# Keeping the two short row blocks of a softmax in the score bank

## The chip, the cores and the metric

The kernel runs on one core of a Trainium2 chip. Five engines work side by side, each through its own instruction queue: TensorE (PE, matrix products and transposes), VectorE (DVE), ScalarE (ACT), GpSimd (POOL) and SyncE (SP, which here issues nearly all transfers from memory). Matrix products land in eight accumulator banks, each 128 partitions by 512 float32 columns; everything else lies in SBUF, the on-chip memory. DVE and ACT can read and write both; POOL touches SBUF alone in this kernel.

The metric is the device time of one execution in microseconds (us). An execution can also be profiled: the profiler then gives the start and the duration of every instruction, and what released each wait.

## The reference

The model is a two-layer decoder trunk on one sequence of 512 tokens, width 1024, with 16 heads of 64 columns. Each layer is an attention block, an output projection with a normalisation, and a gated feed-forward block. The first layer uses a stick-breaking attention, the second a "forgetting" attention, a causal softmax with a learned decay:

```
for blk in range(s_len // Q_BLOCK):           # blocks of 128 queries
    z = einsum('bhqd,bhkd->bhqk', qb, kb) * scale
    decay = cum[:, :, q0:k_end, None] - cum[:, :, None, :k_end]
    logits = where(s_idx <= t_idx, z + decay, -inf)
    p = softmax(logits, axis=-1)
    outs.append(einsum('bhqk,bhkd->bhqd', p, vb))
```

Block `blk` sees 128, 256, 384 or 512 keys, because the attention is causal. The results must agree with float32 arithmetic; the kernel therefore splits operands of its products into a high and a low part, and a projection multiplies three times.

## The kernel before

The attention of a layer is one loop over 17 steps, `attention`. Step h computes scores and probabilities of head h and, at the same time, transposes the probabilities of head h - 1 and multiplies them with its values. Within a step the four query blocks go from the longest row (512 columns) to the shortest (128). Between these pieces PE gets other work in fixed portions, the "filler": the projections of the next heads' queries, keys and values (tiles `pqk` and `pv`), and in the last four steps the first part of the output projection (tile `po`, lines 266 to 268), whose sums stay in banks until the attention is over: two banks for each of the first two row blocks, and two more for the third.

The order of PE and of SP is the order of the program text, written by hand. The order on ACT, DVE and POOL is worked out by a planner when the program is built, from its own estimates of durations. On the chip each engine runs its list strictly in order, and an instruction that waits holds up everything behind it on its engine.

All eight banks come from one ring (tile tag `bank`). A bank is given out again when the last instruction that reads its content is done. SBUF tiles of 512 columns come from a pool of 44 slots (`slot`).

The parts that matter here:

- `scores` (line 388) fills a bank `ps` with the scores of one row block, two products.
- `fox` (lines 403 to 413) makes probabilities of it. DVE adds the decay `cum`, finds the extreme value of each row (`mx`) and writes the sum to an SBUF slot `fx` (line 407). ACT takes the exponential in place in `fx` and sums each row (line 410, the sum is read out by a second small instruction). DVE takes the reciprocal (line 411) and scales `fx` in place (line 412).
- `transposed` (line 422) turns the four blocks by PE into banks `pa`; ACT writes the rounded high part `ah`, DVE the remainder `al` (lines 192 and 193).
- `weighted` (lines 437 and 438) multiplies `ah` and `al` with the values into a bank `po`. ACT and DVE fold its halves together (lines 442 and 443).
- `queries` (lines 359 and 361) and `keys` (lines 377 to 380) prepare the next pair of heads on ACT, DVE and POOL; POOL also makes the low parts of the weights (`wl`, `sl`, line 193) and masks the decay (`cum`, line 502).
- `stick` is the first layer's counterpart of `fox`. There, too, the rows of up to `MULN` = 256 columns stay in their bank (`om = slot("om", F32) if n > MULN else ps`), and DVE's last product on line 400 reads the bank; for the longer rows POOL makes that product, from SBUF.

Of the kernel before, what the change touches and what calls it, by code (L numbers as in the profile page):

```python
# [8 lines left out]
F32 = mybir.dt.float32  # L9
F32R = mybir.dt.float32r  # L10
BF16 = mybir.dt.bfloat16
AF = mybir.ActivationFunctionType
ALU = mybir.AluOpType
AX = mybir.AxisListType

P = 128
# [12 lines left out]
MULN = 256  # L29
# [8 lines left out]
def trunk(ctx, tc, x, c, w_mod, b_mod, g_mix_pre, g_mix_post, w_qkv, w_o, w_fg, b_fg,  # L38
          g_ffn_pre, g_ffn_post, w_gate, w_up, w_conv, b_conv, w_down, out):
    nc = tc.nc  # L40
# [6 lines left out]
    def nm(s):  # L47
        serial[0] += 1
        return f"{s}_{serial[0]}"
# [4 lines left out]
    def slot(s, dt=F32R):  # L54
        return sb.tile([P, 512], dt, tag="slot", name=nm(s), bufs=NS)
# [7 lines left out]
    def tiny(s, n=1):  # L63
        return sb.tile([P, n], F32, tag=f"tiny{n}", name=nm(s), bufs=24)
# [336 lines left out]
        return bt  # L401

    def fox(ps, qb, cum):
        n = (qb + 1) * P
        t = slot("fx", F32)
        m, s, r = tiny("mx"), tiny("sm"), tiny("rc")
        nc.vector.tensor_tensor_reduce(
            t[:, :n].rearrange("p (b k) -> p b k", k=P), ps[:, :n].rearrange("p (b k) -> p b k", k=P), cum(qb),
            1.0, BIG, op0=ALU.add, op1=ALU.min, accum_out=m)
        nc.scalar.activation(t[:, :n], t[:, :n], AF.Exp, scale=-1.0, bias=m, accum_out=s)  # L410
        nc.vector.reciprocal(r, s)
        nc.vector.tensor_scalar(t[:, :n], t[:, :n], r, None, op0=ALU.mult)
        return t

    def transposed(probs):
# [111 lines left out]
    def attention(l, qk, vt, ot, filler, units, bg):  # L527
# [4 lines left out]
        for h in range(NH + 1):  # L532
# [17 lines left out]
            for qb in range(NT - 1, -1, -1):  # L550
                if h < NH:
                    ps, n = scores(l, hd, qb, qk[p, 0], qk[p, 1])
                    probs[qb] = stick(ps, n) if l % 2 == 0 else fox(ps, qb, cums[h])
                    fill()
                if turned:
                    at = next(turned)
                    fill()
# [207 lines left out]
    for l in range(DEPTH):  # L765
        bg = Background([(l, GT_A), (l, SC_F), (l, SH_F)] if l == 0 else [])
        scale = -0.125 if l % 2 else 0.125
# [174 lines left out]
```

## Time and profile before

| quantity | value |
|---|---|
| median of 3 runs | 1309.29 us (1306.78 to 1309.57) |
| the profiled execution's own time | 1307.82 us |
| its span, first to last instruction | 1306.0 us |
| busy share of the span: PE, DVE, ACT, POOL | 96%, 63%, 47%, 21% |
| the second layer's softmax, first to last reduction (line 407) | 711.8 to 899.9 us |

The span is what the profile divides into engines and lines; the 1.8 us that the profiled execution's time has beyond it are its start and end. The profiled execution is 1.5 us below the median of the runs.

In the listings below a row of the timeline gives start, duration, engine, line, operation, the tile written and the tiles read, the shape, and in square brackets the idle time of that engine before it and who ended it. PE's products overlap: a row of 0.39 us is followed by the next start after some 0.23 us.

### The profile page before, as it was taken

To read this page: it belongs to the slowest core of one execution; us is meant where nothing else is said; L and a number is where in the kernel's file an instruction comes from. 1 tells how busy PE (TensorE), PEld (TensorE's weight loads), DVE (VectorE), ACT (ScalarE), POOL (GpSimd) and SP (SyncE) were. 2 spreads that over 40 slices of the span, in tenths; PEclk is the share of its full clock that TensorE was granted. 3 is DMA by queue.
4 is the path that set the end of the run, shared out by engine and by line. 5 is a ranking of instruction groups with operands and counts; after the bars stand their busy time and mean duration, and the time that the engine had idled before them with its cause. 6 is when DMAs were issued, how large, how long until landed. Compare 5 with 4: busy or idle time off the path is not lost.

```text
span 1306.0 us, 17087 instructions
## 1 busy us (share of the span) xinstructions
PE 1249.1 (96%) x6244; PEld 1050.2 (80%) x6244; DVE 818.9 (63%) x1447; ACT 620.0 (47%) x1182; POOL 277.2 (21%) x302
## 2 busy tenths in 40 slices
PE   5898988999999999999999899999999999999997
PEld 3676867789888888888887788887898888888886
DVE  7778888856878887422264776886775444443233
ACT  5576665757433333311365565566753333332121
POOL 3665444530000000000114554443100000000000
PEclk8999989999999999999999999999999999999999
DMA  8662534231577776333503423232263333333331
GB/s 265 208 193 82 168 107 133 94 108 43 189 242 242 246 229 202 97 97 97 164 1 115 130 91 120 81 129 81 66 210 113 97 97 98 97 97 97 97 97 65
DMA packets 174856, 169.19 MB, mean 130 GB/s; under 512 B 6936, under 2 KB 151728, under 8 KB 174772
## 3 DMA queue, kind: packets, MB, share of 16 engines
q1 hardware_dynamic: 174596, 168.04, 41.1%
q8 instruction: 49, 0.80, 0.3%
q14 instruction: 35, 0.29, 0.1%
q10 hardware_dynamic: 176, 0.07, 0.0%
HBM read 165.92 MB, written 2.16 MB: 129 GB/s over the span
## 4 chain that ended last, share of the span: by engine, by line
PE 72%; DVE 14%; ACT 5%; DMA 4%; issue 3%; POOL 1%; SPq 0%; DVEq 0%; POOLq 0%; ACTq 0%
PE pgu L267 11%; PE pgu L268 11%; PE pgu L266 11%; PE pd L268 6%; PE pd L267 6%; PE pd L266 6%; PE pqk L266 2%; DVE acc L143 2%; PE pqk L267 2%; PE pqk L268 2%; PE po L266 2%; PE po L268 2%; PE po L267 2%; PE ps L388 2%; DMA wm<-in_w_mod_dram 2%
## 5 line engine op out<-in xcount | busy, mean ns | idle before, releaser
L192 ACT CAST wh<-wf 128x1024 fp32r<-128x1024 f32 (+2 forms) x178 | 185.3, 1041 | 319.7 <-PE pgu L267 144.0
L193 DVE TENSOR_TENSOR wl<-wf,wh 128x1024 fp32r<-128x1024 f32 x122 | 149.3, 1224 | 217.9 <-ACT wh L192 215.7
L267 PE MATMUL pgu<-htl,wh 128*128 128x512 f32 (+1 forms) x736 | 276.4, 375 | 0.1
L266 PE MATMUL pgu<-hth,wh 128*128 128x512 f32 (+1 forms) x736 | 276.4, 375 | 0.0
L268 PE MATMUL pgu<-hth,wl 128*128 128x512 f32 (+1 forms) x736 | 276.2, 375 | 0.0
L193 POOL TENSOR_TENSOR wl<-wf,wh 128x1024 fp32r<-128x1024 f32 (+3 forms) x56 | 132.5, 2370 | 131.6 <-ACT wh L192 126.4
L267 PEld LDWEIGHTS pgu<-htl,wh 128*128 128x128 f32 x736 | 138.5, 188 | 25.6 <-DVE htl L328 0.5
L268 PEld LDWEIGHTS pgu<-hth,wl 128*128 128x128 f32 x736 | 138.5, 188 | 25.1
L266 PEld LDWEIGHTS pgu<-hth,wh 128*128 128x128 f32 x736 | 138.5, 188 | 24.9
L279 POOL TENSOR_TENSOR r<-v,mhalf 128x1 f32<-128x1 f32 x32 | 17.9, 558 | 447.3 <-DVE v L275 447.3
L266 PE MATMUL pd<-wh,yh 128*128 128x512 f32 x288 | 112.0, 389 | 0.0
L267 PE MATMUL pd<-wl,yh 128*128 128x512 f32 x288 | 112.0, 389 | 0.0
L268 PE MATMUL pd<-wh,yl 128*128 128x512 f32 x288 | 112.0, 389 | 0.0
L143 DVE SCALAR_TENSOR_TENSOR acc<-wm,csil,acc 128x1024 f32<-128x1024 f32 x74 | 99.4, 1344 | 17.1 <-DMA wm<-in_w_mod_dram 16.8
L266 PE MATMUL pqk<-hth,wh 128*128 128x512 f32 (+1 forms) x240 | 101.5, 423 | 0.1
L268 PE MATMUL pqk<-hth,wl 128*128 128x512 f32 (+1 forms) x240 | 94.5, 394 | 0.3 <-POOL wl L193 0.3
L267 PE MATMUL pqk<-htl,wh 128*128 128x512 f32 (+1 forms) x240 | 94.1, 392 | 0.0
L854 ACT ACTIVATE cv<-cv 128x512 f32<-128x512 f32 x44 | 27.8, 632 | 102.7 <-DVE cv L853 98.2
L266 PE MATMUL pv<-wh,hth 128*128 128x256 f32 (+1 forms) x224 | 70.7, 316 | 1.2 <-ACT wh L192 0.8
L267 PE MATMUL pv<-wl,hth 128*128 128x256 f32 (+1 forms) x224 | 67.7, 302 | 1.2 <-POOL wl L193 1.2
L268 PE MATMUL pv<-wh,htl 128*128 128x256 f32 (+1 forms) x224 | 67.9, 303 | 0.0
L266 PEld LDWEIGHTS pd<-wh,yh 128*128 128x128 f32 x288 | 54.1, 188 | 11.3
(194 smaller groups left out, 2459.6 us busy)
## 6 DMA issues: line engine op xcount, KB each, us to landing
wm<-in_w_mod_dram SPq DMA_DIRECT2D x80, 512.0 KB, 4.8
wf<-in_w_ffn_gate_dram SPq DMA_DIRECT2D x44, 512.0 KB, 4.2
wf<-in_w_ffn_up_dram SPq DMA_DIRECT2D x44, 512.0 KB, 3.7
wf<-in_w_ffn_down_dram SPq DMA_DIRECT2D x44, 512.0 KB, 3.5
wf<-in_w_qkv_dram SPq DMA_DIRECT2D x41, 512.0 KB, 3.8
wm<-in_w_mod_dram SPq DMA_DIRECT2D x32, 256.0 KB, 4.3
wf<-in_w_o_dram SPq DMA_DIRECT2D x16, 512.0 KB, 3.8
cum<-cumd SPq DMA_DIRECT2D x16, 512.0 KB, 4.3
```

Of the source, the lines that this page charges most:

```text
L143: nc.vector.scalar_tensor_tensor(acc, w, csil[:, d : d + 1], acc, op0=ALU.mult, op1=ALU.add)
L192: nc.scalar.copy(hi, src)
L193: (engine or nc.vector).tensor_tensor(lo, src, hi.bitcast(F32), op=ALU.subtract)
L266: nc.tensor.matmul(ps, ah, bh, start=first, stop=False)
L267: nc.tensor.matmul(ps, ah, bl, start=False, stop=False)
L268: nc.tensor.matmul(ps, al, bh, start=False, stop=last)
L279: nc.gpsimd.tensor_tensor(r, v, mhalf, op=ALU.pow)
L388: nc.tensor.matmul(ps[:, :n], q[hd][:, qs], k[hd][i][:, :n], start=i == 0, stop=i == 1)
L854: nc.scalar.activation(a, a, AF.Silu)
```

## The change

`fox` gets a second name, `e`, for the place where the sum and the exponential are written. For rows of 512 and 384 columns it is the SBUF slot as before; for rows of 256 and 128 columns it is the score bank itself. DVE's reduction then writes its sum back to the bank it read, ACT's exponential runs in place in the bank, and DVE's scaling reads the bank and writes the SBUF slot.

```diff
     def fox(ps, qb, cum):
+
         n = (qb + 1) * P
-        t = slot("fx", F32)
+        t = slot("fx", F32)[:, :n]
+        e = t if n > MULN else ps[:, :n]
         m, s, r = tiny("mx"), tiny("sm"), tiny("rc")
         nc.vector.tensor_tensor_reduce(
-            t[:, :n].rearrange("p (b k) -> p b k", k=P), ps[:, :n].rearrange("p (b k) -> p b k", k=P), cum(qb),
+            e.rearrange("p (b k) -> p b k", k=P), ps[:, :n].rearrange("p (b k) -> p b k", k=P), cum(qb),
             1.0, BIG, op0=ALU.add, op1=ALU.min, accum_out=m)
-        nc.scalar.activation(t[:, :n], t[:, :n], AF.Exp, scale=-1.0, bias=m, accum_out=s)
+        nc.scalar.activation(e, e, AF.Exp, scale=-1.0, bias=m, accum_out=s)
         nc.vector.reciprocal(r, s)
-        nc.vector.tensor_scalar(t[:, :n], t[:, :n], r, None, op0=ALU.mult)
+        nc.vector.tensor_scalar(t, e, r, None, op0=ALU.mult)
         return t
```

The number of instructions is the same. The scores' bank of a short row is now last read by line 412 instead of line 407. One blank line is added ahead of `n`, and one line for `e`, so that line numbers behind them are higher by two in a profile of the changed kernel.

## The prediction

> **What bounds the kernel now.** I read the page first, then the busy times by stretch, then the groups by shape, then the timeline.
>
> ```profile
> PE 1249.1 (96%) x6244; PEld 1050.2 (80%) x6244; DVE 818.9 (63%) x1447; ACT 620.0 (47%) x1182; POOL 277.2 (21%) x302
> ```
>
> PE bounds the whole. A change on DVE can only gain where PE stands idle for DVE. The stretches (time, then busy us and instructions of PE, PEld, DVE, ACT, POOL, then PE's granted clock) show how much that is in the softmax's stage and behind it:
>
> ```profile
> 711.00:905.00 194.00, 185.20 (x1076) 159.41 (x1075) 147.60 (x382) 119.62 (x283) 94.23 (x76) 0.99 0.37 115
> 905.00:1290.00 385.00, 385.00 (x1808) 323.13 (x1807) 179.24 (x224) 142.85 (x219) 7.67 (x12) 1.00 0.33 102
> ```
>
> In the stage PE is idle for 194.00 - 185.20 = 8.8 us: the ceiling of any gain but for the clock. Behind it PE is never idle, so what PE gains in the stage arrives at the end unshortened, and nothing there waits for a transfer that could swallow it.
>
> Where the 8.8 us lie, by PE's timeline (idle time and releaser in brackets):
>
> ```profile
> 731.84 0.33 PE L437 MATMUL po<-ah,v 128*128 128x128 f32 x1 [1.34 <-ACT ah L192]
> 734.35 0.33 PE L438 MATMUL po<-al,v 128*128 128x128 f32 x1 [2.19 <-DVE al L193]
> 760.81 0.33 PE L438 MATMUL po<-al,v 128*128 128x128 f32 x1 [0.40 <-DVE al L193]
> 786.33 0.33 PE L438 MATMUL po<-al,v 128*128 128x128 f32 x1 [1.32 <-DVE al L193]
> 836.44 0.33 PE L438 MATMUL po<-al,v 128*128 128x128 f32 x1 [0.73 <-DVE al L193]
> 881.76 0.39 PE L438 MATMUL po<-al,v 128*128 128x256 f32 x1 [0.88 <-DVE al L193]
> 883.07 0.33 PE L438 MATMUL po<-al,v 128*128 128x128 f32 x1 [0.86 <-DVE al L193]
> ```
>
> These seven make 7.72 us, and six of them end with DVE's `al`. So the question is what made DVE late. By shape, the scaling on line 412 is odd:
>
> ```profile
> L412 DVE TENSOR_SCALAR fx<-fx,rc 128x256 f32<-128x256 f32 x16 | 14.1, 880 | 0.2
> L412 DVE TENSOR_SCALAR fx<-fx,rc 128x512 f32<-128x512 f32 x16 | 13.2, 824 | 0.2
> L412 DVE TENSOR_SCALAR fx<-fx,rc 128x128 f32<-128x128 f32 x16 | 12.2, 762 | 0.5
> L412 DVE TENSOR_SCALAR fx<-fx,rc 128x384 f32<-128x384 f32 x16 | 8.9, 556 | 0.1
> ```
>
> 256 columns take longer in the mean than 384. The timeline shows why; here is the short rows' scaling beside POOL, undisturbed and not:
>
> ```profile
> 729.04 0.35 DVE L412 TENSOR_SCALAR fx<-fx,rc 128x256 f32<-128x256 f32 x1
> 870.17 0.29 DVE L412 TENSOR_SCALAR fx<-fx,rc 128x128 f32<-128x128 f32 x1
> 730.15 2.35 POOL L193 TENSOR_TENSOR wl<-wf,wh 128x1024 fp32r<-128x1024 f32 x1 [1.68 <-issue]
> 731.12 1.46 DVE L412 TENSOR_SCALAR fx<-fx,rc 128x128 f32<-128x128 f32 x1
> 782.05 2.41 POOL L193 TENSOR_TENSOR wl<-wf,wh 128x1024 fp32r<-128x1024 f32 x1 [3.99 <-ACT wh L192]
> 782.59 1.95 DVE L412 TENSOR_SCALAR fx<-fx,rc 128x128 f32<-128x128 f32 x1
> ```
>
> A scaling that starts while POOL runs ends just after POOL's instruction: 732.58 after 732.50, 784.54 after 784.46. DVE stands still for POOL. Operations of DVE with one operand in a bank and one in SBUF do not (minimum, median and maximum in ns):
>
> ```profile
> L193 DVE TENSOR_TENSOR al<-pa,ah x128: 266/475/694, 86.6 to 904.4; 128x512 fp32r<-128x512 f32 x32, 128x384 fp32r<-128x384 f32 x32, 128x256 fp32r<-128x256 f32 x32, 128x128 fp32r<-128x128 f32 x32
> L400 DVE TENSOR_TENSOR bt<-bt,ps x32: 264/344/421, 80.2 to 263.8; 128x255 f32<-128x255 f32 x16, 128x127 f32<-128x127 f32 x16
> L412 DVE TENSOR_SCALAR fx<-fx,rc x64: 275/480/2668, 713.9 to 900.7; 128x512 f32<-128x512 f32 x16, 128x384 f32<-128x384 f32 x16, 128x256 f32<-128x256 f32 x16, 128x128 f32<-128x128 f32 x16
> ```
>
> Four lengths of `al` span 266 to 694 ns with no outlier in 128, over stages with POOL busy; line 400, which writes SBUF from a bank and a slot, is as steady.
>
> **The change part by part.** It adds no instruction and moves none to another queue; no transfer is issued earlier or later by it. *Scaling from the bank.* No row shows a scaling that reads a bank. Its neighbours do: line 400 reads a bank over 255 and 127 columns, at 421 and 264 ns at the ends. I take 0.41 and 0.28 us for 256 and 128 columns. From below the bound is the undisturbed 0.35 and 0.29, from above today's means. DVE's time falls by 16 x (0.880 - 0.41) + 16 x (0.762 - 0.28) = 15.2 us of 147.6; undisturbed instances cost 0.06 more at 256 columns, at most 1 us over 16.
>
> The Trainium skill ("VectorE: DVE Perf Modes", section "Why PSUM operands drop a tier") speaks against the edit: float32 from a bank runs in the plain mode, from SBUF at double rate. By that alone, DVE would have more work, by the 1 us just worked out, and nothing would be gained; the two undisturbed rows against line 400 agree that the loss is that small.
>
> *Reduction into the bank, exponential in the bank.* Same instructions; the reduction already reads the bank. Between a loss of 0.1 and a gain of 0.1 us each, I take nothing: PE waits on neither directly, only through the chain below.
>
> *What PE gains*, wait by wait. The first two (step 1 of the loop) hang on this chain on DVE:
>
> ```profile
> 716.47 1.82 DVE L412 TENSOR_SCALAR fx<-fx,rc 128x256 f32<-128x256 f32 x1
> 718.39 2.24 DVE L412 TENSOR_SCALAR fx<-fx,rc 128x128 f32<-128x128 f32 x1
> 719.81 1.19 ACT L377 CAST kh<-pqk 64x512 fp32r<-64x512 f32 x2
> 722.09 1.40 DVE L380 TENSOR_TENSOR kl<-pqk,kh 64x512 fp32r<-64x512 f32 x2
> 734.01 0.29 DVE L193 TENSOR_TENSOR al<-pa,ah 128x128 fp32r<-128x128 f32 x1
> ```
>
> The first two scalings shrink by 1.41 and 1.96 us. Late next is ACT's `kh`: with its first half at 720.4 `kl` can start there, not at 722.09, so DVE's list moves up by 1.7 us. The scaling at 731.12 shrinks by another 1.18. `al` of 734.01 thus comes 2.9 us earlier, PE's product likewise, and both waits shrink from 3.53 to some 0.6: **2.9 us**. Bounds: 1.18 (the list ahead doesn't move) and 3.53.
>
> After these waits the clock sank; after the 1.32 us at 786.33 it didn't:
>
> ```profile
> 734.30:738.00 3.70, 3.65 (x11) 2.86 (x12) 1.38 (x3) 0.78 (x2) 1.43 (x2) 0.59 0.66 197
> 784.00:808.00 24.00, 22.68 (x166) 21.33 (x165) 17.02 (x43) 13.41 (x30) 10.05 (x10) 1.00 0.30 93
> ```
>
> At 0.59 over 3.70 us PE lost 3.70 x 0.41 = 1.5 us. A remaining wait of 0.6 us should leave the clock alone; I take **1.2** between 0 and 1.5.
>
> At 760.81 (0.40) the scaling of 128 columns before it took 1.37, at 786.33 (1.32) 1.95, at 836.44 (0.73) one of 256 columns took 1.91:
>
> ```profile
> 758.86 1.37 DVE L412 TENSOR_SCALAR fx<-fx,rc 128x128 f32<-128x128 f32 x1
> 832.00 1.91 DVE L412 TENSOR_SCALAR fx<-fx,rc 128x256 f32<-128x256 f32 x1
> 881.63 0.98 DVE L412 TENSOR_SCALAR fx<-fx,rc 128x256 f32<-128x256 f32 x1
> ```
>
> Each shrinks by more than its wait (1.09, 1.67, 1.50): **0.4 + 1.3 + 0.7**. At 883.07 the scaling at 881.63 gives **0.5** of 0.86. The 0.88 at 881.76 stays: longer rows lie before it, which the change leaves in SBUF. Their scalings go on meeting POOL, at other moments; I count no change. Sum of gains: 2.9 + 1.2 + 2.4 + 0.5 = 7.0.
>
> *What the longer hold costs.* The bank of a short row comes free after the scaling instead of the reduction. Behind a PE instruction that waits for a bank everything on PE waits. While the ring is slack this is free; from about 880 us on the output projection's sums sit in up to four of the eight banks, later in six, and it is not:
>
> ```profile
> 887.55 0.33 PE L388 MATMUL ps<-kh,qa 128*128 128x128 f32 x1 [0.21 <-DVE mx L407]
> 888.80 0.08 DVE L407 DVE_READ_ACCUMULATOR2_ANT mx<- 128x1 f32 x1
> 889.38 0.40 PE L437 MATMUL po<-ah,v 128*128 128x512 f32 x1
> 889.95 0.35 DVE L412 TENSOR_SCALAR fx<-fx,rc 128x256 f32<-128x256 f32 x1
> ```
>
> At 887.55 PE already waits for a reduction to free a bank. The product at 889.38 would find the 256-column row's bank held until 890.3 instead of 888.88, 0.9 us too long, unless a turned block's bank comes free first. The last three heads have six short rows; most of their banks have a later user. I take **-1.0**, between 0 and six holds of 1.4 us, -8.4.
>
> The first layer keeps its short rows so already; of PE's waits in its last steps, 230 to 270 us, the one for DVE is small:
>
> ```profile
> PE ps L388 <- DVE om L399: 0.7, 1, 0.7
> ```
>
> Net 7.0 - 1.0 = 6.0 us. The profiled execution, 1307.8 us, becomes 1301.8; it stood 1.5 below the median, so I forecast **1303.3 us**, 0.5% faster.
>
> **The rivals.** *Another wait takes the place* (chance 0.18, about 1308): DVE is early, but ACT's `ah`, a long row's scaling or a new order of the planner, which re-sorts ACT, DVE and POOL with changed durations, holds PE as long. For it: the 1.34 us on ACT. Against: the chain above goes through line 412. Gaining only the certain 1.18 gives 1309.3 - 1.2.
>
> *The scaling still stands still* (0.04, 1309), if POOL blocks writes to SBUF and not the second reading. Line 400 speaks against it.
>
> *The bank ring* (0.12, slower): all six holds fall on PE, 8.4 us, the planner's order lets them grow to 2 us (12 us), and the gain ahead, 6.5, is eaten: 1309.3 + 12 - 6.5 = 1314.8. It decides once the holds cost more than 6.5 + 2.6. For it: the wait at 887.55. Against: 0.7 us in the first layer.
>
> **How the numbers follow.** The forecast case holds 0.66: its own range is from 1309.3 - 8.8 - 1.5 = 1299 (every idle moment and the clock) to 1306.5. A measurement tells about 0.2%, 2.6 us, from no change. Faster: 0.68, the forecast and a little of the first rival; same: 0.20; slower: 0.12. The range runs to 1311, past both cases without change.
>
> **What would show it.** Right: line 412's short rows near 0.41 and 0.28 with no outlier; the waits at 731.84 to 836.44 nearly gone, the clock full near 735; PE idle for 3 us in the stage, not 8.8. Wrong: scalings of short rows still stretched; new waits of PE released by line 412 in the last four steps; or the same waits of `al` behind other instructions.

## The result and the profile after

| | before | changed |
|---|---|---|
| median of 6 runs | 1309.43 us (1306.59 to 1310.66) | 1299.85 us (1295.07 to 1302.55) |
| ratio, 95% interval | | 0.993 (0.9907 to 0.9953) |
| span of the profiled execution | 1306.0 us | 1293.3 us |

The change gains 0.7%, some 9.2 us (between 6.2 and 12.2 by the interval). 1303.3 was forecast, within 1299 to 1311. The profiled execution of the changed kernel happens to be its quickest run, so that the spans differ by 12.7 us. Not all of it is the change: the first and the last row of the score products (line 388, by head parity; behind the counts come the durations in ns and the first and last start) show the stage itself. Before, then after:

```profile
L388 PE MATMUL ps<-kh,qa x32: 221/333/632, 704.6 to 887.5; 128*128 128x512 f32 x8, 128*128 128x384 f32 x8, 128*128 128x256 f32 x8, 128*128 128x128 f32 x8
L388 PE MATMUL ps<-kl,qb x32: 272/311/398, 719.5 to 896.5; 128*128 128x512 f32 x8, 128*128 128x384 f32 x8, 128*128 128x256 f32 x8, 128*128 128x128 f32 x8
```

```profile
L388 PE MATMUL ps<-kh,qa x32: 221/330/502, 700.9 to 872.7; 128*128 128x512 f32 x8, 128*128 128x384 f32 x8, 128*128 128x256 f32 x8, 128*128 128x128 f32 x8
L388 PE MATMUL ps<-kl,qb x32: 272/311/397, 715.8 to 883.0; 128*128 128x512 f32 x8, 128*128 128x384 f32 x8, 128*128 128x256 f32 x8, 128*128 128x128 f32 x8
```

The changed execution reaches the stage 3.7 us sooner, before any changed instruction has run: that is no effect of the change. From the first to the last score product it takes 883.0 - 700.9 = 182.1 us instead of 896.5 - 704.6 = 191.9, which is 9.8 us less and agrees with the ratio.

The busy times by stretch, for the stage and what lies behind it:

```profile
711.00:892.30 181.30, 179.09 (x1061) 155.01 (x1060) 130.65 (x376) 116.53 (x280) 90.97 (x71) 1.00 0.37 116
892.30:1276.00 383.70, 383.36 (x1801) 321.74 (x1800) 178.34 (x222) 142.56 (x219) 7.49 (x11) 1.00 0.34 102
```

PE is idle for 2.2 us in the stage, not 8.8, its clock is full throughout, and the part behind is as dense as before. The groups of the scaling, by shape:

```profile
L414 DVE TENSOR_SCALAR fx<-fx,rc 128x512 f32<-128x512 f32 x16 | 11.9, 746 | 0.2
L414 DVE TENSOR_SCALAR fx<-fx,rc 128x384 f32<-128x384 f32 x16 | 9.5, 591 | 0.1
L414 DVE TENSOR_SCALAR fx<-ps,rc 128x256 f32<-128x256 f32 x16 | 7.7, 480 | 0.1
L414 DVE TENSOR_SCALAR fx<-ps,rc 128x128 f32<-128x128 f32 x16 | 5.5, 344 | 0.1
```

The short rows fall from 880 and 762 ns to 480 and 344; the long rows, still in SBUF, keep means well above their undisturbed time. The timeline of DVE and POOL in the first step shows one of the short scalings under a POOL instruction that runs from 712.09 to 716.85:

```profile
712.91 0.48 DVE L414 TENSOR_SCALAR fx<-ps,rc 128x256 f32<-128x256 f32 x1
714.13 0.35 DVE L414 TENSOR_SCALAR fx<-ps,rc 128x128 f32<-128x128 f32 x1
712.09 4.76 POOL L193 TENSOR_TENSOR wl<-wf,wh 128x1024 fp32r<-128x1024 f32 x2 [1.90 <-ACT wh L192]
```

The same two scalings took 1.82 and 2.24 us before, beside the same two POOL instructions. What is left of PE's waits from 700 to 893 us, in us, times, longest, but for two more of 0.2 us:

```profile
PE ps L388 <- POOL kh L379: 1.4, 1, 1.4
PE pa L424 <- DVE al L193: 0.6, 1, 0.6
PE po L266 <- DVE kl L380: 0.5, 1, 0.5
PE pqk L268 <- POOL wl L193: 0.4, 1, 0.4
PE ps L388 <- DVE mx L409: 0.2, 1, 0.2
```

The first lies at the very start of the stage and was there before. Between 715 and 866 us PE waits for nothing.

### The profile page after: what moved, and what is told of

Same layout as the page of the kernel before. It is cut to its first block, busy times and chain, and to the rows that moved or that the text cites. A ratio compares the mean times of both kernels' runs of the same rounds, so it can differ in the third digit from the quotient of the medians.

```text
span 1293.3 us, 17081 instructions
## 1 busy us (share of the span) xinstructions
PE 1245.4 (96%) x6244; PEld 1048.1 (81%) x6244; DVE 801.4 (62%) x1447; ACT 618.4 (48%) x1182; POOL 277.7 (21%) x302
## 4 chain that ended last, share of the span: by engine, by line
PE 74%; DVE 12%; ACT 5%; DMA 4%; issue 3%; POOL 2%; SPq 0%; DVEq 0%; POOLq 0%; ACTq 0%
PE pgu L267 11%; PE pgu L266 11%; PE pgu L268 11%; PE pd L266 6%; PE pd L268 6%; PE pd L267 6%; PE pqk L266 3%; PE pqk L268 3%; PE pqk L267 3%; PE ps L388 2%; PE pa L424 2%; DMA wm<-in_w_mod_dram 2%; PE pv L267 2%; PE pv L266 2%; PE pv L268 2%
## 5 line engine op out<-in xcount | busy, mean ns | idle before, releaser
L192 ACT CAST ah<-pa 128x128 fp32r<-128x128 f32 (+3 forms) x128 | 53.7, 427 | 21.0 <-PE pa L424 20.3
```

The source lines that it names most:

```text
L192: nc.scalar.copy(hi, src)
```

## The experiments

The theory: the gain comes from the short rows' scalings, which no longer stand still while GpSimd works. The rivals: a better order on ACT and DVE, since the planner sorted both anew; the shorter exponential (in the bank 446 and 344 ns instead of 510 and 401); and, against the gain, the longer hold of the banks. The experiments ran in two rounds, and each ratio is to the kernel before as it ran in the same round: a median of 1308.03 us for the first four below, 1307.39 us for the others.

**The scaling alone, in the old order.** `fx` gets its slot at the reduction as before, the exponential writes the bank, the scaling reads it; ACT and DVE issue the second softmax in the order of the kernel before (the diff is shortened).

```diff
-        nc.scalar.activation(t[:, :n], t[:, :n], AF.Exp, scale=-1.0, bias=m, accum_out=s)
+        e = t if n > MULN else ps
+        nc.scalar.activation(e[:, :n], t[:, :n], AF.Exp, scale=-1.0, bias=m, accum_out=s)
         nc.vector.reciprocal(r, s)
-        nc.vector.tensor_scalar(t[:, :n], t[:, :n], r, None, op0=ALU.mult)
+        nc.vector.tensor_scalar(t[:, :n], e[:, :n], r, None, op0=ALU.mult)
...
+    for names in ORDER.values():          # the old order, ACT and DVE
+        for a, b in zip(names, names[1:]):
+            tc.add_manual_dep(traced[b], a, ..., reason="order")
```

> The kernel before, with one thing changed for the rows of 256 and 128 columns: the exponential reads the slot as before but writes the bank, and the scaling reads the bank. The order of all instructions on ScalarE and VectorE is held to that of the kernel before. Theory (the gain comes from scalings that no longer stand still for GpSimd): nearly the whole gain, some 1300 us, ratio to before 0.991 to 0.996, short scalings at 0.48 and 0.34 us without outliers. Rival (the gain comes from the new order that the planner made): 1309, ratio 0.998 to 1.002, since the order is the old one.

Measured: 1301.72 us, ratio 0.995 (0.9929 to 0.9971), short scalings at 481 and 350 ns. The scaling alone gives most of the gain with no help of the order. What it doesn't give shows in the first steps. Its PE timeline, and its DVE timeline and clock there:

```profile
732.73 0.33 PE L438 MATMUL po<-ah,v 128*128 128x128 f32 x1 [1.29 <-ACT ah L192]
734.18 0.33 PE L439 MATMUL po<-al,v 128*128 128x128 f32 x1 [1.13 <-DVE al L193]
```

```profile
725.56 2.63 DVE L413 TENSOR_SCALAR fx<-fx,rc 128x512 f32<-128x512 f32 x1
732.00 0.35 DVE L413 TENSOR_SCALAR fx<-ps,rc 128x128 f32<-128x128 f32 x1
```

```profile
730.00:736.00 6.00, 3.58 (x17) 2.82 (x16) 3.81 (x10) 3.21 (x7) 3.25 (x3) 1.00 0.65 190
```

The two waits are 2.42 us, not 3.53, and not the 0.6 of the forecast: a scaling of 512 columns met POOL for longer (2.63 us, 1.66 before) and took back what the short ones had freed. The clock stayed full all the same. In the changed kernel both waits are gone. There ACT and DVE make the last `ah` and `al` of the step ahead of the queries' preparation (`qa`, `qb`), which the old order has the other way round. DVE in the changed kernel, then in the old order:

```profile
725.39 0.29 DVE L193 TENSOR_TENSOR al<-pa,ah 128x128 fp32r<-128x128 f32 x1
726.48 0.68 DVE L361 SCALAR_TENSOR_TENSOR qa<-pqk,qa 64x512 fp32r<-64x512 f32 x1 [0.54 <-ACT qb L359]
```

```profile
732.42 0.69 DVE L361 SCALAR_TENSOR_TENSOR qa<-pqk,qa 64x512 fp32r<-64x512 f32 x1
733.84 0.29 DVE L193 TENSOR_TENSOR al<-pa,ah 128x128 fp32r<-128x128 f32 x1
```

The times of the two kernels (0.995 and 0.993, intervals overlapping) don't tell the order's share from nothing; the traces put it at the 2.4 us of these two waits. That the order took them, and not the other moments at which the long scalings met POOL or the reduction that here still writes the slot, is argued; the run with the 256-column row alone (below) supports it.

**All but the scaling.** Reduction in the bank, exponential from the bank to the slot, scaling in the slot.

```diff
-        nc.scalar.activation(e, e, AF.Exp, scale=-1.0, bias=m, accum_out=s)
+        nc.scalar.activation(t, e, AF.Exp, scale=-1.0, bias=m, accum_out=s)
         nc.vector.reciprocal(r, s)
-        nc.vector.tensor_scalar(t, e, r, None, op0=ALU.mult)
+        nc.vector.tensor_scalar(t, t, r, None, op0=ALU.mult)
```

> The changed kernel with the scaling alone undone for the short rows: the reduction writes the bank, the exponential reads the bank and writes the slot, the scaling reads and writes the slot. The planner orders as it likes. Theory (scalings that stand still): the gain is gone, 1309, ratio 0.997 to 1.002, and short scalings are stretched again up to about 2 us. Rivals (a freer order because the reduction needs no slot; shorter exponentials): 1300 to 1303, ratio 0.993 to 0.996.

Measured: 1307.02 us, ratio 0.9999 (0.9979 to 1.002). The gain is gone whole, and the stretched scalings are back, as the groups show, with the two waits of the first step:

```profile
L414 DVE TENSOR_SCALAR fx<-fx,rc 128x256 f32<-128x256 f32 x16 | 14.2, 890 | 0.1
L414 DVE TENSOR_SCALAR fx<-fx,rc 128x128 f32<-128x128 f32 x16 | 12.5, 782 | 0.5
```

```profile
730.41 0.33 PE L439 MATMUL po<-ah,v 128*128 128x128 f32 x1 [1.22 <-ACT ah L192]
732.87 0.47 PE L440 MATMUL po<-al,v 128*128 128x128 f32 x1 [2.14 <-DVE al L193]
```

The clock behind these waits was at half for some 7 us, 3.4 in the kernel before. The short rows' exponentials took 473 and 376 ns here, less than the 510 and 401 before, and nothing was gained: that rival is out. A reduction that needs no slot, and the order that the planner made of it here, gain nothing by themselves. That order isn't the changed kernel's: in the first step the stretched scaling still lies ahead of the last `al`.

**The other side of the standstill.** The kernel before, but POOL works on 256 columns at a time in the second softmax (the lines that set `cut` there are left out).

```diff
         nc.scalar.copy(hi, src)
+        if engine is nc.gpsimd and cut:
+            for c in range(0, lo.shape[-1], 256):
+                cs = slice(c, c + 256)
+                engine.tensor_tensor(lo[:, cs], src[:, cs], hi.bitcast(F32)[:, cs], op=ALU.subtract)
+            return
         (engine or nc.vector).tensor_tensor(lo, src, hi.bitcast(F32), op=ALU.subtract)
```

> The kernel before, all scalings in the slot, but GpSimd makes the low parts of the weights in the second softmax in pieces of 256 columns instead of 1024 or 512. Theory (scalings wait for the GpSimd instruction that runs): a standstill lasts at most some 0.65 us instead of 2.4, the 23.7 us over all four lengths fall to about a quarter, and most of the gain comes without the change: 1300 to 1303, ratio 0.993 to 0.996. If scalings were late for another reason: 1309 or, with more instructions on GpSimd, slower.

Measured: 1299.07 us, ratio 0.9935 (0.9911 to 0.996): a gain of the same size, and not a line of the softmax is changed. By shape, the scaling and POOL's pieces:

```profile
L419 DVE TENSOR_SCALAR fx<-fx,rc 128x512 f32<-128x512 f32 x16 | 10.1, 630 | 0.2
L419 DVE TENSOR_SCALAR fx<-fx,rc 128x256 f32<-128x256 f32 x16 | 8.8, 547 | 0.2
L419 DVE TENSOR_SCALAR fx<-fx,rc 128x128 f32<-128x128 f32 x16 | 5.7, 359 | 0.5
L198 POOL TENSOR_TENSOR wl<-wf,wh 128x256 fp32r<-128x256 f32 x84 | 60.6, 752 | 36.5 <-ACT wh L194 32.8 <-PE pa L429 3.4
```

The exponentials are as long as before (509 and 401 ns). Scalings still wait for a piece, but a piece lasts 0.75 us instead of 2.4. In POOL's own time the pieces are dearer (four make 3.0 us), which nobody waits for here.

**The hold alone.** The kernel before, plus a one-column copy out of the bank behind each short row's scaling.

```diff
         nc.vector.tensor_scalar(t[:, :n], t[:, :n], r, None, op0=ALU.mult)
+        if n <= MULN:
+            nc.vector.tensor_copy(tiny("hd"), ps[:, :1])
```

> The kernel before, plus a copy of one column out of the bank right behind the scaling of each short row (32 small copies, some 2 us of VectorE in all): the bank is held as long as in the changed kernel, and nothing else of the change is there. Forecast's term (the hold costs 1.0 us): 1309 to 1312, ratio 1.000 to 1.002. Rival (the ring of banks decides): 8 us more, ratio 1.006, with TensorE waits released by this copy in the last four steps.

Measured: 1312.3 us, ratio 1.003 (1.001 to 1.0049), by the ratio some 3.9 us slower: more than the forecast's term, less than the rival's, and no wait of PE ends with the copy. The trace has one new wait for a bank, that of the output projection, and twice a clock at half speed (its stretches give the clock in the third place from the end):

```profile
885.49 0.50 PE L266 MATMUL po<-wh,oh 128*128 128x512 f32 x1 [1.06 <-DVE kl L380]
```

```profile
733.00:741.00 8.00, 6.13 (x18) 5.03 (x19) 4.41 (x10) 2.33 (x5) 1.42 (x3) 0.57 0.49 145
839.00:843.00 4.00, 3.43 (x9) 2.79 (x10) 1.94 (x6) 0.58 (x1) 1.21 (x2) 0.57 0.96 275
```

The new wait of 1.06 us ends with `kl`, the last reader of a projection's bank. The kernel before has no wait at this product; the changed kernel and the old-order run, which hold the score banks too, have 0.45 and 0.31 us there, but the run with both remedies (below), which also holds them, has none. So the 1.1 us go with the hold; that it sends the product to another bank is argued, not shown. Much of the rest is the clock: at most 8 x 0.43 + 4 x 0.43 = 5.2 us of PE's speed lost in these two stretches against 1.5 in the kernel before. Its second fall came with three waits of 0.43, 0.70 and 0.80 us within 2.7 us, ahead of the products at 837.36, 838.44 and 839.57. Why the waits grew was not tried apart; the 32 copies lie in the chain that was late already.

**More rows in the bank.** All four rows, and then three (512 columns stay in the slot).

```diff
-        e = t if n > MULN else ps[:, :n]
+        e = ps[:, :n]                          # all four
+        e = t if n > 384 else ps[:, :n]        # three
```

> The changed kernel with all four rows kept in the bank. From the short rows' 0.344 and 0.480 us, 0.136 more for each 128 columns, the long scalings should take 0.62 and 0.75 us, near today's means of 0.59 and 0.75, but without outliers. Theory (waits of TensorE come from single long standstills, not from VectorE's total): the last waits for al go, 1 to 2 us better than the changed kernel, ratio to before 0.990 to 0.993. Rival (the ring of banks): with every row's bank held until its scaling, TensorE waits for banks in the last four steps and part of the gain is given back, ratio 0.994 to 0.999.

> The changed kernel with the rows of 384, 256 and 128 columns kept in the bank, only those of 512 in the slot. Theory: between the changed kernel and the one with all rows in the bank, ratio 0.990 to 0.994; the scaling of 384 columns at 0.62 us without outliers. Rival (ring of banks): worse than the changed kernel, ratio 0.994 to 0.998.

Measured: all four 1302.14 us, ratio 0.9955 (0.9939 to 0.9971); three 1308.17 us, ratio 0.9996 (0.9976 to 1.0016), its single runs from 1301.27 to 1311.33 us. Here the ring of banks decides. With three rows, PE's timeline in the last steps, DVE and POOL ahead of the first of the waits, and the clock behind each of them:

```profile
871.77 0.33 PE L424 MATMUL pa<-zid,fx 128*128 128x128 f32 x1 [2.55 <-DVE fx L414]
883.36 0.39 PE L388 MATMUL ps<-kh,qa 128*128 128x128 f32 x1 [2.21 <-DVE fx L414]
895.60 0.33 PE L388 MATMUL ps<-kh,qb 128*128 128x128 f32 x1 [1.82 <-DVE fx L414]
```

```profile
868.32 2.47 DVE L414 TENSOR_SCALAR fx<-fx,rc 128x512 f32<-128x512 f32 x1
871.11 0.61 DVE L414 TENSOR_SCALAR fx<-ps,rc 128x384 f32<-128x384 f32 x1
868.14 2.36 POOL L193 TENSOR_TENSOR wl<-wf,wh 128x1024 fp32r<-128x1024 f32 x1
```

```profile
873.00:877.00 4.00, 4.00 (x13) 3.23 (x12) 2.27 (x6) 2.90 (x8) 3.22 (x5) 0.57 0.07 26
883.00:887.00 4.00, 3.64 (x11) 2.92 (x12) 2.49 (x10) 1.48 (x6) 0.00 (x0) 0.57 0.01 2
897.00:901.00 4.00, 4.00 (x13) 3.28 (x12) 1.08 (x4) 0.87 (x3) 1.79 (x2) 0.57 0.30 89
```

In the first of them the bank of the 384-column row waits for its scaling, which lies behind the 512-column scaling, which stands still for POOL: the old stall reaches PE again, through a bank. Ahead of the third wait the 512-column scaling took 1.57 us. Ahead of the second it took 0.48 us and did not stand still; there DVE itself came late, after 3.00 us of idle time that ended with POOL's `sl` at 878.32. Three waits of 1.8 to 2.6 us, each followed by a half-speed clock (4 x 0.43 = 1.7 us each), eat the gain. With all four rows no scaling stands still (749, 614, 480 and 344 ns), but PE still waits for banks in the last steps, and for a filler's bank once:

```profile
PE pa L424 <- DVE of L445: 1.7, 1, 1.7
PE ps L388 <- DVE fx L414: 2.3, 3, 0.8
PE pqk L266 <- DVE fx L414: 1.0, 1, 1.0
```

The expectation for all four had the scaling's time right; its theory had the sign of the rest wrong, and the rival that it names is what the trace shows. The interval overlaps with the changed kernel's, so the times alone don't show a loss against it. Three rows came out beyond both ranges that were expected.

**The row of 256 columns alone.**

```diff
-        e = t if n > MULN else ps[:, :n]
+        e = t if n != 256 else ps[:, :n]
```

> The changed kernel with only the row of 256 columns kept in the bank; the row of 128 is scaled in the slot as before. By the forecast's terms, the waits at 731.84, 734.35, 760.81 and 786.33 of the kernel before hang on scalings of 128 columns, at least in part, and 836.44 and 883.07 on 256. Theory: about a third to a half of the gain, 1304 to 1306, ratio 0.996 to 0.998. Rival (the terms are wrong and one row carries it all): 0.993 or 1.000.

Measured: 1302.06 us, ratio 0.995 (0.9929 to 0.9971), more than the third to a half that was expected, though the interval reaches into that range and the 128-column scaling still averages 701 ns. DVE's timeline of the first step shows what the expectation left out:

```profile
728.74 0.28 DVE L193 TENSOR_TENSOR al<-pa,ah 128x128 fp32r<-128x128 f32 x1
729.58 0.92 DVE L414 TENSOR_SCALAR fx<-fx,rc 128x128 f32<-128x128 f32 x1
```

The planner put the last `al` ahead of the 128-column scaling and of `qa`, as in the changed kernel, and both first waits are gone. All stretched 128-column scalings of this run that share a step with an `al` (0.92 to 1.93 us) lie behind it. In the kernel before, three of them (1.46, 1.37 and 1.95 us) lie ahead of the `al` that PE waits for at 734.35, 760.81 and 786.33. So part of this run's gain is the order's: a standstill costs PE nothing where nothing that PE needs lies behind it. An order like this with all scalings in the slot was not run.

**Both remedies.** The changed kernel with POOL's pieces.

> The changed kernel, and GpSimd makes the low parts of the weights in the second softmax in pieces of 256 columns. The long rows' scalings, which still stand still for GpSimd, then wait some 0.65 us at most. Theory: both remedies act on the same standstill, so that they don't add up: the changed kernel's ratio of 0.993, at best 1 to 2 us better (0.991 to 0.994). Rival (the pieces gain by something else, such as earlier weights): the gains add up, ratio 0.985 to 0.989.

Measured: 1296.37 us, ratio 0.9916 (0.9894 to 0.9938), the lowest of all; the intervals overlap with those of either remedy alone. The gains don't add up (the sum would be a ratio near 0.987), which fits two remedies for the same standstill. Its scalings in SBUF, by shape, are now shorter too:

```profile
L421 DVE TENSOR_SCALAR fx<-fx,rc 128x512 f32<-128x512 f32 x16 | 10.5, 658 | 0.2
L421 DVE TENSOR_SCALAR fx<-fx,rc 128x384 f32<-128x384 f32 x16 | 8.0, 502 | 0.1
```

The 746 and 591 ns of the changed kernel become 658 and 502; PE, with few waits left there, has little use for it.

## Why the prediction was right, and where its sizes were off

*The scaling stands still for POOL, and not when it reads a bank.* Right: shown by the old-order run (0.995), by its counterpart without the scaling (0.9999) and by POOL's pieces (0.9935). The forecast put 0.41 and 0.28 us; it is 0.48 and 0.34. DVE was relieved of 13.1 us instead of 15.2, which changes nothing at the waits of 760.81, 786.33 and 836.44, where each scaling still shrank by more than the wait behind it.

*The waits at 760.81, 786.33 and 836.44* (2.4 us): right, all gone in the changed kernel; in the old order 0.23 us of the second is left, at 782.91.

*The first two waits* (2.9 us of 3.53): near in sum, wrong in its working, so that the sum is luck. By the scalings alone 1.1 us went, about the forecast's lower bound, the case in which the list ahead doesn't move. The forecast let `kl` start after the first half of `kh`. In the old-order run `kl` starts at 722.00, when both halves are done (they start at 720.78 and take 1.19 us). PE reaches this place 1.0 us later in that run (719.17 against 718.19 for the same product), so DVE's list had moved up by 1.1 us, not by 1.7, and the 512-column scaling took that back. The new order took the other 2.4 us, as far as the traces tell, so 3.5 in all. The forecast had treated the planner's order as a risk only.

*The clock* (1.2 us): right; it was full at that point, with 2.42 us of waits left in the old order as well as with none. The forecast's reason, that a short wait leaves the clock alone, is not borne out: in the run with the hold alone the clock fell with waits of 0.43, 0.70 and 0.80 us close together.

*The waits at 881.76 and 883.07* (0.5 us of 1.74): too small, 0.17 us is left of them, at 868.23. The forecast left the first wait as it was, because it counted the long rows' meetings with POOL as unchanged. In the changed kernel the two long scalings ahead took 1.59 and 0.61 us instead of 1.78 and 0.82, and PE came later itself, behind its new wait of 0.45 us for a bank. These are other moments of the same meetings, luck and no term of the change.

*The bank's hold* (-1.0 us): of the right size, as far as the traces tell. The changed kernel has two new waits for a bank in the last steps, 0.45 us at 866.98 and 0.57 at 874.48; the hold alone showed 1.06. None of them ends with the scaling, as the forecast pictured it, but with the last reader of another bank (`kl`, `al`), and the run with all but the scaling has the second one too (0.56 us).

*The sum* (6.0 us against 9.2): right in sign and place, a third too small, just outside the interval (6.2 to 12.2). Beside the first two waits (3.5 us for 2.9) and the last two (1.6 for 0.5), a term was missing that the kernel before already shows. The idle time in brackets starts when a product's row ends, but the next product could have started sooner. Undisturbed, and before the wait at 786.33:

```profile
890.42 0.23 PE L437 MATMUL po<-ah,v 128*128 128x128 f32 x1
890.49 0.27 PE L438 MATMUL po<-al,v 128*128 128x128 f32 x1
784.78 0.22 PE L437 MATMUL po<-ah,v 128*128 128x128 f32 x1
```

The pair normally starts 0.07 us apart; at 784.78 and 786.33 it is 1.55, so the wait cost PE 1.48 us where the bracket says 1.32. The same working gives 0.15 to 0.26 us more than the bracket for each of the six waits ahead of line 438, 1.1 us together, so the "ceiling" of 8.8 us was some 1 us too low. With these corrections, and 1.5 us for 1.2 at the clock, the sum would be 9.1 us; the interval is too wide to confirm it.

*The rivals.* Another wait in place of the old: did not come, PE's idle time fell by 6.6 us. The scaling still standing still: refuted by its groups. The ring of banks: not at two rows, but real at three, where the gain is gone, in the steps and by the releaser that the forecast had named.

## What to carry to other kernels

Where a group's mean is out of line with its size, look at its slowest instances beside the other engines' timelines: an instruction that ends again and again just after another engine's may be waiting for it, and still counts as busy. Then either side can be mended, here by reading the operand from a bank or by cutting the blocker in pieces, and the two don't add up. Ask also what lies behind the stretched instruction: in the run with the 256-column row alone the order took part of the cost away. A buffer held longer cost about 1 us with two rows and the whole gain with three; count the ring where it is fullest, and see what its release lies behind.

## What was not expected of the hardware

The scaling out of a bank is slower than another DVE operation with a bank operand: 480 ns for 256 columns against 421 for the product of line 400 over 255. The read-out of the row extreme on DVE after a reduction into a bank took 0.14 us instead of 0.08. PE's clock fell to half, for about 3.4 us, after single waits of 1.8 to 2.6 us in the run with three rows, and with waits of 0.43, 0.70 and 0.80 us within 2.7 us in the run with the hold alone, but not after two waits of 1.29 and 1.13 us within 2.8 us in the old-order run. These runs give no length of wait from which the clock falls.
